# Two layers of a three-branch diffusion backbone: merging the branches straight from PSUM, and the last modulation tiles computed by matrix products

## The chip, the cores and the metric

The kernel runs on one core of one Trainium2 chip. The metric is device time in microseconds (us) of one execution, median of several runs. Smaller is better. The engines are called by the names of the profile: PE is TensorE's matmul, PEld its weight load, DVE is VectorE, ACT is ScalarE, POOL is GpSimd, SP is SyncE, which here only issues DMAs.

## The reference, cut to what matters

Per layer (there are two), on 640 tokens of 1024 channels (128 context tokens, 512 latent tokens):

```python
mod = jnp.einsum('bd,de->be', jax.nn.silu(cond), p['w_mod']) + p['b_mod']
sh1, sc1, g1, sh2, sc2, g2 = jnp.split(mod[:, None, :], 6, axis=-1)
h = rms_norm(x, p['norm1']) * (1 + sc1) + sh1
u_f, q_g, k_g, v_g, r_g, a_g, q_d, k_d, v_d, gates = split_projection(h @ p['w_in'])
y_f = fourier_mix(u_f) @ p['w_fou']
...
y_g = o_g.reshape(b, t, GLA_V) @ p['w_gla_o']
...
y_d = o_d.reshape(b, t, DIFF_V) @ p['w_diff_o']
gf, gg, gd = jnp.split(jax.nn.sigmoid(gates), N_BRANCH, axis=-1)
merged = gf * y_f + gg * y_g + gd * y_d
x = x + g1 * (merged @ p['w_out'])
h2 = rms_norm(x, p['norm2']) * (1 + sc2) + sh2
ff = (jax.nn.silu(h2 @ p['w_ff_gate']) * (h2 @ p['w_ff_up'])) @ p['w_ff_down']
x = x + g2 * ff
```

`mod` has 48 tiles of 128 numbers for each of two conditions (context and latent tokens).

## The kernel before

**Products.** All activations lie channel-major: a tile has 128 channels in the partitions and 640 tokens, cut into two halves of 320 (`SPLIT`). Each float32 operand is split into a high and a low part, and a product is three matmuls (high x high, low x high, high x low). So a gate tile (1024 input channels) is 8 x 3 = 24 matmuls of 320 columns for each half (`group`), and a branch's output tile (512 input channels) is 12. Their results go to the PSUM tiles `main`, of which there are two. A third matmul group can start only when the first one's `main` tile has been read for the last time.

**Weights.** SP loads a raw half unit (L403), ACT rounds it to the high part (L450), POOL subtracts to get the low part (L454). `used` frees a half unit and at once starts this chain for a later one, so a new raw load waits until POOL has emptied a raw buffer.

**The branches' merge.** The mixer runs branch 0 (Fourier), 1 (gated linear attention) and 2 (differential attention). In branches 0 and 1, `branch` alternates for each of 8 output tiles: gate tile (two groups of 24 matmuls, tanh by ACT at L1417), then `merge` (two groups of 12). In branch 2 all 8 gate tiles come first and then all 8 merges. `merge` copies the product out of PSUM with ACT (`y`, L1426); DVE then multiplies by the gate (L1428 in branch 0, L1430 in the others) and, in the others, adds to `merged` (L1431). In branch 2 the sum is also split for the next product: ACT rounds it (`mh`, L485), DVE subtracts (`ml`, L486). The next product is `w_out`, whose first group needs all 8 tiles `mh` of one half.

**Side work.** Attention, linear attention and the Fourier transform are Python generators; `slot(columns)` is called after each group and steps them, so their PE instructions lie between the groups and their DVE instructions are handed out among the merge's.

**Modulation.** A second generator, `back`, is stepped every `rate` columns of main work. Tiles 0 to 15 of a layer are matrix products (`mod_first`, L734, four 32-column parts of the array at once, then a transpose at L743). Tiles 16 to 47 are dot products on DVE: `mod_next` loads `cond_b` (4 DMAs), applies silu to it, and then for each tile loads two half rows (L774) and runs two multiply-and-sum instructions on each (L781) and a final add (L785). In the mixer of layer 0 it makes tiles 16 to 35 and then, from the gates of branch 2 on, 36 to 47 at a rate of 128; in layer 1 it makes 32 to 47 there at a rate of 256. `finish_back` runs what is left of a generator at once.

**Order.** PE's instructions stay in the order in which the program writes them, everywhere (`ORDERED`). From `w_out` to the end of a layer DVE, ACT and POOL do too. In the mixer a planner with its own cost table orders DVE, ACT, POOL and SP; each engine then runs that list in order, and an instruction that waits holds up those behind it.

Of the kernel before, what the change touches and what calls it, by code (L numbers as in the profile page):

```python
# [17 lines left out]
ALU = mybir.AluOpType  # L18
# [4 lines left out]
P = 128  # L23
D = 1024
DEPTH = 2
# [4 lines left out]
KT = D // P  # L30
# [14 lines left out]
UNITS = 58  # L45

AHEAD = 6
ORDERED = {mybir.EngineType.PE}
FFN_ORDERED = {mybir.EngineType.DVE, mybir.EngineType.Activation, mybir.EngineType.Pool}
STEP = 250  # L50
# [73 lines left out]
def weight_jobs():  # L124
# [3 lines left out]
    for l in range(DEPTH):  # L128
        u, pairs = U_FF, set()
        for fp, (_, n) in enumerate(FF_PARTS):  # L130
            pairs.update(range(u + (0 if fp else AHEAD), u + 2 * n, 2))
            u += 3 * n
# [19 lines left out]
def pack_mod(w):  # L152

    return w[:, :2048].reshape(KT, P, 2, 4, 256).transpose(3, 0, 1, 2, 4).reshape(32, P, 512)


def pack_modt(w):

    return w.T.reshape(48, P, 2, 512).transpose(0, 2, 1, 3).reshape(96, P, 512)
# [58 lines left out]
S_N1, S_N2, S_BM, S_GLA, S_DIF = 0, 8, 16, 64, 192  # L218
# [5 lines left out]
def _rows(*vs):  # L224
    return np.concatenate([np.broadcast_to(v.reshape(1, -1), (P, v.size)) for v in vs], 1)


def pack_small(i, l):
    return np.concatenate(
        [  # L230
            i["norm1"][l].reshape(KT, P).T,
            i["norm2"][l].reshape(KT, P).T,
            i["b_mod"][l].reshape(48, P).T,
            _rows(i["gla_norm"][l], i["diff_norm"][l]),
        ],
        1,
    )


def pack_dif(i, l):  # L240
    half = np.arange(64).reshape(2, 2, 16)[:, ::-1].reshape(64)
    gq, gk = i["diff_qk_norm"][l]
    return _rows(gq, gq[half], gk, gk[half], i["diff_lambda"][l])


def pack_a2(i, l):


    w = i["w_gla_a2"][l]
    a, b = np.zeros((P, 4, P), w.dtype), np.zeros((P, 4, P), w.dtype)  # L250
    for pr in range(2):
        for d in range(2):
            s = slice(pr * P, pr * P + P)
            for r in range(d * 16, P, 32):
                a[r : r + 16, pr * 2 + d] = w[d][:, s]
            b[:64:32, pr * 2 + d] = i["b_gla_a"][l][d, s]
    return np.concatenate([a, b])


def layout(i):  # L260
    i = {k: np.asarray(v) for k, v in i.items()}
    x = np.concatenate([i["x_prompt"][0], i["x_sample"][0]], 0)
    cond = np.stack([i["c_ctx"], i["c"][0]], 1)
    return {
        "x_t": np.ascontiguousarray(x.T),
        "cond": np.ascontiguousarray(cond.reshape(KT, P, 2).transpose(1, 0, 2)),
        "w": np.stack([u for l in range(DEPTH) for u in pack_layer(i, l)]),
        "cond_b": np.broadcast_to(cond.T.reshape(1, 2, D), (P, 2, D)),
        "w_mod": np.concatenate([pack_mod(i["w_mod"][l]) for l in range(DEPTH)]),
        "w_modt": np.concatenate([pack_modt(i["w_mod"][l])[32:] for l in range(DEPTH)]),  # L270
        "small": np.stack([pack_small(i, l) for l in range(DEPTH)]),
        "dif": np.stack([pack_dif(i, l) for l in range(DEPTH)]),
        "a2": np.stack([pack_a2(i, l) for l in range(DEPTH)]),

        "ck": np.concatenate([i["cache_diff_k"][0].reshape(DEPTH, P, 2, 4, 64).transpose(0, 2, 4, 3, 1)] * 2, 2),
        "cv": np.ascontiguousarray(i["cache_diff_v"][0].reshape(DEPTH, P, 512)),
        "s0": np.ascontiguousarray(
            i["state_gla"][0].reshape(DEPTH, 2, 2, 2, 64, P).transpose(0, 3, 4, 2, 1, 5).reshape(DEPTH, P, 2, 2, P)
        ),
        **CONST,  # L280
    }
# [23 lines left out]
class Kernel:  # L305
# [446 lines left out]
    def mod_next(self, l, m0, m1, small, mod):  # L752

        nc = self.nc
        cond = {}
        for i in range(2):
            for k in range(2):
                cond[i, k] = self.unit("cond")[:, :512]
                nc.sync.dma_start(cond[i, k], self.a["cond_b"][:, i, k * 512 : (k + 1) * 512])
        yield  # L760
        ends = collections.deque()
        for i, k in [(i, k) for i in range(2) for k in range(2)] + [(None, None)]:
            if i is not None:
                ends.append(self.silu(cond[i, k], self.unit("cond_t")[:, :512]))
            if i is None or len(ends) > 1:
                ends.popleft()()
            yield
        todo = [(m, k) for m in range(m0, m1) for k in range(2)]
        raws = collections.deque()
        for n in range(len(todo) + 2):  # L770
            if n < len(todo):
                m, k = todo[n]
                raws.append(self.unit("rawm")[:, :512])
                nc.sync.dma_start(raws[-1], self.a["w_modt"][l * 64 + m * 2 + k - 32])  # L774
            if n >= 2:
                m, k = todo[n - 2]
                raw = raws.popleft()
                if k == 0:
                    sums = self.sm([P, 2, 2], "modsum", 3)
                for i in range(2):  # L780
                    nc.vector.scalar_tensor_tensor(  # L781
                        self.sm([P, 512], "junk", 1, mybir.dt.bfloat16), raw, 1.0, cond[i, k], op0=ALU.mult, op1=ALU.mult, accum_out=sums[:, i, k : k + 1]
                    )
                if k:
                    nc.vector.scalar_tensor_tensor(mod[:, m], sums[:, :, 0], small[:, S_BM + m : S_BM + m + 1], sums[:, :, 1], op0=ALU.add, op1=ALU.add)  # L785
            yield

    def mod_scale(self, mod, small, gain, tile0, name):

        o = self.lp.tile([P, KT, 2], F32, tag=name, name=self.name(name), bufs=2)  # L790
        for i in range(2):
            self.nc.vector.scalar_tensor_tensor(
                o[:, :, i], mod[:, tile0 : tile0 + KT, i], 1.0, small[:, gain : gain + KT], op0=ALU.add, op1=ALU.mult
            )
        return o
# [624 lines left out]
    def merge(self, l, u, m, act, tg, merged, first=False, parts=None):  # L1420

        nc = self.nc
        for s in SPLIT:
            ps = self.group(self.weight(l, u), (m % 2) * 4, 4, act, s)
            y = self.unit("y")[:, s]
            nc.scalar.copy(y, ps)  # L1426
            if first:
                nc.vector.scalar_tensor_tensor(merged[m][:, s], tg[:, s], 1.0, y, op0=ALU.add, op1=ALU.mult)  # L1428
            else:
                nc.vector.scalar_tensor_tensor(tg[:, s], tg[:, s], 1.0, y, op0=ALU.add, op1=ALU.mult)  # L1430
                nc.vector.tensor_add(merged[m][:, s], merged[m][:, s], tg[:, s])  # L1431
            if parts:
                self.split(merged[m][:, s], parts[0][:, s], parts[1][:, s])
            if m % 2 and s.start:
                self.used(l, u)
            self.slot((s.stop - s.start) // 2)
# [43 lines left out]
    def mixer(self, l, h, small, backs, norms):  # L1480
        nc = self.nc
# [38 lines left out]
        for s in SPLIT:  # L1520
            ps = self.main()[:, : s.stop - s.start]
# [9 lines left out]
        for i, r in enumerate((slice(0, P), slice(P, 2 * P))):  # L1531
            raw, x = (self.unit("a2", t)[:, :512] for t in (F32, F32R))
# [6 lines left out]
        for pr in range(2):  # L1539
            k, q, vs = self.qkv(l, pr, h)  # L1540
# [13 lines left out]
        for pr in range(2):  # L1554
# [14 lines left out]
            if pr == 0:  # L1569
                merged = [self.unit("mg") for _ in range(KT)]  # L1570
# [2 lines left out]
                self.finish(gens[1])  # L1573
                self.branch(l, 1, h, gact, merged)
        self.finish_back()
        self.back, self.rate = backs[1], 128 if l == 0 else 256
        tg = [self.gate(l, U_BR[2] + m, h) for m in range(KT)]
        self.finish(gens[3])
        mg, x2 = self.pairs("m", KT), [self.unit("x2") for _ in range(KT)]
# [7 lines left out]
    def ffn_start(self, l, h2, combine, norms, pair):  # L1587

        us = range(U_FF, U_FF + AHEAD)
        first, second = self.first_four(l, us[:4], h2, norms)  # L1590
        acts = [pair(f) for f in range(AHEAD // 2)]
        for f in range(2):
# [16 lines left out]
        self.used(l, us[2])  # L1609
        for i in range(4, AHEAD):  # L1610
            for p in range(2):
# [86 lines left out]
    def run(self):  # L1698
        nc = self.nc
        self.load_consts()  # L1700
        small, mod = self.load_small(0)
# [3 lines left out]
        with self.tc.manual_schedule(engines={mybir.EngineType.SP}):  # L1705
# [6 lines left out]
            raws = [self.mod_load(0)]  # L1712
# [7 lines left out]
        h = self.pairs("h", KT)  # L1720
        todo = collections.deque()
# [50 lines left out]
        norms = None  # L1772
        for l in range(DEPTH):
            last = l == DEPTH - 1
            if l:
                small, mod = later[l - 1]
            later_mod = lambda a, b: self.mod_next(l, a, b, small, mod)
            mg, x2 = self.mixer(l, h, small, (None, later_mod(32, 48)) if l else (later_mod(16, 36), later_mod(36, 48)), norms)

            g1 = self.lp.tile([P, KT, 2], F32, tag="g1", name=self.name("g1"), bufs=1)  # L1780
            nc.vector.tensor_scalar_mul(g1, mod[:, 16:24, :], 0.5)
# [5 lines left out]
            norms = []  # L1787
# [8 lines left out]
            with self.tc.manual_schedule(engines=FFN_ORDERED):  # L1796
                for m, p in NORM_ORDER:
                    s = SPLIT[p]
# [17 lines left out]
            first, keep, norms = norms, [], []  # L1816
# [13 lines left out]
            h = keep[0]  # L1830
# [3 lines left out]
def hybrid_dit_kernel(ctx: ExitStack, tc: tile.TileContext, a):  # L1834
    with tc.manual_schedule(engines=ORDERED):
        Kernel(ctx, tc, a).run()
# [34 lines left out]
```

## Time and profile before

| | |
|---|---|
| median of 3 runs | 2377.06 us (2373.94 to 2380.15) |
| the profiled execution's own time | 2375.32 us |
| its span, first to last instruction | 2373.5 us |
| PE busy | 2236.4 us, 94% of the span |
| DVE busy | 1639.4 us, 69% |
| ACT busy | 996.0 us, 42% |
| POOL busy | 976.0 us, 41% |
| mean granted TensorE clock | 0.978 of full speed |

PE is the engine that is nearly always busy, so time is lost where PE waits and spent where PE is given more work. The others count where they make PE wait.

### The profile page before, as it was taken

What the parts mean: (1) busy time and instruction counts of PE and PEld (TensorE: products, weight loads), DVE (VectorE), ACT (ScalarE), POOL (GpSimd) and SP (SyncE); (2) the same over time, 40 slices, a digit from 0 to 9 for tenths busy, and PEclk for the clock granted to TensorE, in tenths of its full rate; (3) what the DMA queues carried; (4) which work ended last, traced back from release to release, by engine and by line L of the source; (5) the groups of instructions that cost most, each with busy time, mean ns of one, the idle gap of its engine ahead of it and who ended that gap; (6) DMA issues with size and microseconds to landing.
All of it is one profiled execution on the core that took longest, in us unless ns stands there. A gap on an engine that the chain in (4) does not pass through costs nothing. (4 is left out here: it accounts for less than half of the span.)

```text
span 2373.5 us, 44461 instructions
## 1 busy us (share of the span) xinstructions
PE 2236.4 (94%) x16882; PEld 2187.4 (92%) x16882; DVE 1639.4 (69%) x3386; ACT 996.0 (42%) x2194; POOL 976.0 (41%) x795
## 2 busy tenths in 40 slices
PE   6988899999999899998989999999998998999999
PEld 4978799999999899998989899999998988999999
DVE  5796877686955857778763657867748667575674
ACT  3444445454235424241434554464633254242332
POOL 1344544353333634342533545524433255252533
PEclk9999999999999999999999999999999999999999
DMA  7443221112622272836242222212135322424433
GB/s 269 161 128 102 72 74 59 56 57 76 222 84 81 87 246 85 274 111 211 88 142 72 79 72 72 70 37 76 50 108 182 129 90 74 158 93 162 138 103 125
DMA packets 151381, 271.39 MB, mean 114 GB/s; under 512 B 19200, under 2 KB 31360, under 8 KB 151168
## 3 DMA queue, kind: packets, MB, share of 16 engines
q1 hardware_dynamic: 125824, 219.75, 28.4%
q10 hardware_dynamic: 25344, 48.80, 5.9%
q8 instruction: 133, 2.18, 0.4%
q14 instruction: 80, 0.66, 0.1%
HBM read 235.98 MB, written 27.79 MB: 111 GB/s over the span
## 5 line engine op out<-in xcount | busy, mean ns | idle before, releaser
L454 POOL TENSOR_TENSOR wl<-raw,wh 128x512 fp32r<-128x512 f32 x514 | 707.6, 1391 | 1055.8 <-ACT wh L450 890.1
L450 ACT CAST wh<-raw 128x512 fp32r<-128x512 f32 x518 | 314.9, 619 | 295.6 <-PE main L492 161.9
L492 PE MATMUL main<-hh,wh 128*128 128x320 f32 x936 | 294.9, 315 | 0.8 <-DVE aT L1526 0.8
L492 PE MATMUL main<-hh,wl 128*128 128x320 f32 x936 | 289.5, 309 | 0.0
L492 PE MATMUL main<-hl,wh 128*128 128x320 f32 x936 | 289.5, 309 | 0.0
L492 PE MATMUL main<-wh,hh 128*128 128x256 f32 x800 | 236.8, 296 | 9.0 <-DVE rx L1472 4.9
L781 DVE SCALAR_TENSOR_TENSOR junk<-rawm,cond 128x512 bf16<-128x512 f32 x256 | 222.8, 870 | 27.6 <-DMA rawm<-in_w_modt_dram 22.8
L492 PE MATMUL main<-wl,hh 128*128 128x256 f32 x800 | 230.8, 289 | 0.0
L492 PE MATMUL main<-wh,hl 128*128 128x256 f32 x800 | 230.7, 288 | 0.0
L492 PE MATMUL main<-ah,wh 128*128 128x320 f32 x704 | 219.9, 312 | 7.0 <-DVE x L1453 5.4
L1453 DVE SCALAR_TENSOR_TENSOR x<-main,g,x 128x128 f32<-128x128 f32 (+2 forms) x240 | 97.3, 435 | 185.9 <-PE main L492 170.6
L492 PE MATMUL main<-al,wh 128*128 128x320 f32 x704 | 217.5, 309 | 0.0
L492 PE MATMUL main<-ah,wl 128*128 128x320 f32 x704 | 217.5, 309 | 0.0
L450 ACT CAST wh<-big 128x512 fp32r<-128x512 f32 x152 | 89.2, 587 | 261.1 <-DVE big L433 74.6
L492 PEld LDWEIGHTS main<-hh,wh 128*128 128x128 f32 x936 | 176.4, 188 | 1.6 <-DVE aT L1526 1.0
L492 PE MATMUL main<-h2h,wh 128*128 128x320 f32 x520 | 165.8, 319 | 12.7 <-DVE tt L297 6.3
L492 PEld LDWEIGHTS main<-hl,wh 128*128 128x128 f32 x936 | 176.4, 188 | 0.1
L492 PEld LDWEIGHTS main<-hh,wl 128*128 128x128 f32 x936 | 176.0, 188 | 0.0
L492 PEld LDWEIGHTS main<-wh,hh 128*128 128x128 f32 x800 | 158.3, 198 | 11.8 <-DVE rx L1472 5.1
L492 PE MATMUL main<-h2l,wh 128*128 128x320 f32 x520 | 164.6, 317 | 0.0
L492 PE MATMUL main<-h2h,wl 128*128 128x320 f32 x520 | 164.5, 316 | 0.0
L492 PEld LDWEIGHTS main<-wl,hh 128*128 128x128 f32 x800 | 158.2, 198 | 0.0
(359 smaller groups left out, 6152.7 us busy)
## 6 DMA issues: line engine op xcount, KB each, us to landing
raw<-in_w_dram SPq DMA_DIRECT2D x556, 256.0 KB, 2.9
rawm<-in_w_modt_dram SPq DMA_DIRECT2D x128, 256.0 KB, 4.6
x<-xd ACTq DMA_DIRECT2D x64, 320.0 KB, 4.5
rawm<-in_w_mod_dram SPq DMA_DIRECT2D x64, 256.0 KB, 5.4
xd<-x ACTq DMA_DIRECT2D x48, 320.0 KB, 4.1
xd<-x ACTq DMA_DIRECT2D x48, 160.0 KB, 2.0
cond<-in_cond_b_dram SPq DMA_DIRECT2D x16, 256.0 KB, 4.5
x<-in_x_t_dram SPq DMA_DIRECT2D x12, 320.0 KB, 5.1
```

The lines of the kernel that those rows point to most:

```text
L450: nc.scalar.copy(h, raw)
L454: (nc.vector if late or sums else nc.gpsimd).tensor_sub(lo, raw, h.bitcast(F32))
L492: mm = lambda w, x, first=False, last=False: nc.tensor.matmul(ps, w, x, start=first and not more, stop=last, skip_group_check=more)
L781: nc.vector.scalar_tensor_tensor(self.sm([P, 512], "junk", 1, mybir.dt.bfloat16), raw, 1.0, cond[i, k], op0=ALU.mult, op1=ALU.mult, accum_ ...
L1453: nc.vector.scalar_tensor_tensor(x[:, r], ps[:, r.start - s.start : r.stop - s.start], g[:, m, i : i + 1], x[:, r], op0=ALU.mult, op1=ALU.add)
```

## The change

`merge` no longer copies: DVE multiplies the gate with the PSUM tile itself. In branch 0 it writes `merged`; in branches 1 and 2 it writes the product back into the same PSUM tile and then adds that to `merged`. Tiles 36 to 47 of layer 0 and 32 to 47 of layer 1 become matrix products in a new generator, `mod_rows`, with weights in a new layout (`w_modr`). Four tiles take two halves of four loads (256 KB each) and 16 matmuls each, then a copy by ACT and a transpose. The rate from the gates of branch 2 on is 640 in both layers.

```diff
+MOD_ROWS = (36, 32)
+MOD_BLOCKS = tuple((48 - m) // 4 for m in MOD_ROWS)
...
+    def mod_rows(self, l, m0, m1, small, mod):
+        nc = self.nc
+        todo = [(m, half) for m in range(m0, m1, 4) for half in range(2)]
+        raws = collections.deque()
+        for n in range(len(todo) + 1):
+            if n < len(todo):
+                m, half = todo[n]
+                raws.append([self.unit("rawm")[:, :512] for _ in range(4)])
+                for k, raw in enumerate(raws[-1]):
+                    nc.sync.dma_start(raw, self.a["w_modr"][((m - m0) // 4 + sum(MOD_BLOCKS[:l])) * KT + 4 * half + k])
+                yield
+            if n:
+                m, half = todo[n - 1]
+                if half == 0:
+                    ps = self.misc()
+                for k, raw in enumerate(raws.popleft()):
+                    for j in range(4):
+                        nc.tensor.matmul(
+                            ps[32 * j : 32 * j + 32, :P], self.cond[:, 4 * half + k, :], raw[:, j * P : (j + 1) * P],
+                            start=(half + k == 0), stop=(half == 1 and k == 3),
+                        )
+                if half:
+                    row = self.sm([P, P], "row", 2)
+                    nc.scalar.copy(row, ps[:, :P])
+                    yield
+                    ps = self.misc()
+                    nc.tensor.transpose(ps[:, :P], row, self.c("ident"))
+                    src = ps[:, :P].rearrange("p (m i) -> p m i", m=4)[:, :, :2]
+                    nc.vector.tensor_add(mod[:, m : m + 4], src, small[:, S_BM + m : S_BM + m + 4, None].to_broadcast([P, 4, 2]))
+                yield
...
             ps = self.group(self.weight(l, u), (m % 2) * 4, 4, act, s)
-            y = self.unit("y")[:, s]
-            nc.scalar.copy(y, ps)
             if first:
-                nc.vector.scalar_tensor_tensor(merged[m][:, s], tg[:, s], 1.0, y, op0=ALU.add, op1=ALU.mult)
+                nc.vector.scalar_tensor_tensor(merged[m][:, s], tg[:, s], 1.0, ps, op0=ALU.add, op1=ALU.mult)
             else:
-                nc.vector.scalar_tensor_tensor(tg[:, s], tg[:, s], 1.0, y, op0=ALU.add, op1=ALU.mult)
-                nc.vector.tensor_add(merged[m][:, s], merged[m][:, s], tg[:, s])
+                nc.vector.scalar_tensor_tensor(ps, tg[:, s], 1.0, ps, op0=ALU.add, op1=ALU.mult)
+                nc.vector.tensor_add(merged[m][:, s], ps, merged[m][:, s])
...
-        self.back, self.rate = backs[1], 128 if l == 0 else 256
+        self.back, self.rate = backs[1], 640
...
-            later_mod = lambda a, b: self.mod_next(l, a, b, small, mod)
-            mg, x2 = self.mixer(l, h, small, (None, later_mod(32, 48)) if l else (later_mod(16, 36), later_mod(36, 48)), norms)
+            first_mod = self.mod_next(l, 16, MOD_ROWS[l], small, mod) if l == 0 else None
+            mg, x2 = self.mixer(l, h, small, (first_mod, self.mod_rows(l, MOD_ROWS[l], 48, small, mod)), norms)
```

## Rows read from the trace of the kernel before

**Rows 1.** The page, busy time of each engine.
```profile
PE 2236.4 (94%) x16882; PEld 2187.4 (92%) x16882; DVE 1639.4 (69%) x3386; ACT 996.0 (42%) x2194; POOL 976.0 (41%) x795
```

**Rows 2.** PE's waits, whole span: who waited for whom, total us, times, longest.
```profile
PE main L492 <- ACT y L1426: 14.9, 11, 3.8
...
PE big L1340 <- POOL q L1324: 6.4, 4, 1.7
...
PE main L492 <- ACT mh L485: 5.2, 2, 4.1
...
PE big L1282 <- DVE kT L1238: 3.1, 2, 1.5
```

**Rows 3.** Busy time by stretch: us, PE, PEld, DVE, ACT, POOL, granted clock, DMA.
```profile
639.65:676.70 37.05, 31.27 (x194) 29.69 (x193) 31.46 (x62) 16.19 (x38) 11.61 (x9) 0.95 0.33 111
...
1807.65:1848.52 40.87, 31.68 (x194) 29.72 (x193) 36.05 (x82) 15.61 (x37) 11.50 (x9) 0.96 0.47 159
1848.52:1864.00 15.48, 11.43 (x58) 10.78 (x57) 12.74 (x35) 2.69 (x6) 1.38 (x1) 0.78 0.60 213
...
1751.50:1807.50 56.00, 56.00 (x383) 56.00 (x383) 36.66 (x67) 18.10 (x36) 21.20 (x16) 1.00 0.48 162
```

**Rows 4.** DVE in order of time, the last merge of layer 1: start, duration.
```profile
1853.92 0.48 DVE L1430 SCALAR_TENSOR_TENSOR tg<-tg,y 128x320 f32<-128x320 f32 x1
1854.33 0.68 DVE L781 SCALAR_TENSOR_TENSOR junk<-rawm,cond 128x512 bf16<-128x512 f32 x1
...
1854.94 0.48 DVE L1431 TENSOR_TENSOR mg<-mg,tg 128x320 f32<-128x320 f32 x1
```

**Rows 5.** Groups of DVE instructions by shape: count, busy us, mean ns, idle before.
```profile
L781 DVE SCALAR_TENSOR_TENSOR junk<-rawm,cond 128x512 bf16<-128x512 f32 x256 | 222.8, 870 | 27.6 <-DMA rawm<-in_w_modt_dram 22.8
...
L1430 DVE SCALAR_TENSOR_TENSOR tg<-tg,y 128x320 f32<-128x320 f32 x64 | 41.5, 652 | 7.8 <-ACT y L1426 7.7
L1431 DVE TENSOR_TENSOR mg<-mg,tg 128x320 f32<-128x320 f32 x64 | 38.2, 601 | 1.2
```

**Rows 6.** The instructions of L595: ns min/median/max, first and last start.
```profile
L595 DVE SCALAR_TENSOR_TENSOR tt<-tt,main x38: 475/477/478, 809.0 to 2331.2; 128x320 f32<-128x320 f32 x38
```

**Rows 7.** Modulation matmuls between others, then at the start of the kernel.
```profile
865.54 0.31 PE L492 MATMUL main<-ah,wl 128*128 128x320 f32 x1
865.78 1.08 PE L734 MATMUL misc<-rawm,cond 128*32 128x128 f32 x32
866.79 0.41 PE L492 MATMUL main<-ah,wh 128*128 128x320 f32 x1
...
19.65 0.65 PE L734 MATMUL misc<-rawm,cond 128*32 128x128 f32 x8
...
20.69 0.47 PE L743 MATMUL misc<-const,row 128*128 128x128 f32 x1 [0.39 <-ACT row L740]
```

**Rows 8.** SP at the end of layer 1's merges; DMAs there: KB, us to landing.
```profile
1852.46 0.33 SPq L403 DMA_DIRECT2D raw<-in_w_dram  x1
1852.88 4.11 SPq L774 DMA_DIRECT2D rawm<-in_w_modt_dram  x8
...
rawm<-in_w_modt_dram SPq DMA_DIRECT2D x8, 256.0 KB, 4.4
```

**Rows 9.** DVE's merge instruction and PE's next gate: first, worst, last late pair.
```profile
325.31 0.31 PE L492 MATMUL main<-hh,wh 128*128 128x320 f32 x1
...
325.50 0.48 DVE L1428 SCALAR_TENSOR_TENSOR mg<-tg,y 128x320 f32<-128x320 f32 x1
...
359.50 0.39 PE L492 MATMUL main<-hh,wh 128*128 128x320 f32 x1
...
366.84 0.47 DVE L1428 SCALAR_TENSOR_TENSOR mg<-tg,y 128x320 f32<-128x320 f32 x1
...
1739.85 0.49 DVE L1431 TENSOR_TENSOR mg<-mg,tg 128x320 f32<-128x320 f32 x1
...
1740.23 0.31 PE L492 MATMUL main<-hh,wh 128*128 128x320 f32 x1
```

More of the change, by code (lines that the diff above doesn't have):

```diff
@@ L154, in pack_mod, with pack_modr @@
     return w[:, :2048].reshape(KT, P, 2, 4, 256).transpose(3, 0, 1, 2, 4).reshape(32, P, 512)
+def pack_modr(w, m0):
+    return w[:, P * m0 :].reshape(KT, P, -1, 512).transpose(2, 0, 1, 3).reshape(-1, P, 512)
 def pack_modt(w):
@@ L270, in layout @@
         "w_modt": np.concatenate([pack_modt(i["w_mod"][l])[32:] for l in range(DEPTH)]),
+        "w_modr": np.concatenate([pack_modr(i["w_mod"][l], MOD_ROWS[l]) for l in range(DEPTH)]),
         "small": np.stack([pack_small(i, l) for l in range(DEPTH)]),
```

## Prediction

> **What bounds the kernel now.** I read the page first: PE is busy 94% of the span, DVE 69%, ACT 42% [rows 1]. So a us is won only where PE waits, and each matmul that is added costs its own time. Next come PE's waits by cause [rows 2]: the merge's ACT copy costs 14.9 us in 11 waits, and the rounding `mh` at the start of `w_out` 5.2 in two. Narrowed to stretches, all of both lies in the merges of branch 2 and just behind them; in branches 0 and 1 PE waits for the merge nowhere. There the two waits on side work appear, 6.4 and 3.1 us over both layers.
>
> Then the stretches [rows 3]. Branch 2's gates, at full clock and without a wait, take 56.0 us for 16 groups of 24 matmuls, the last row of the group; its merges are 16 groups of 12 and would need half, 28.0 us. They take 37.05 us in layer 0 and 40.87 in layer 1: 9.0 + 12.8 = 21.8 us lost, part of it at a reduced granted clock (0.95 and 0.96 over the stretch). Behind them come the 5.2 us for `mh`, about 1.4 in short steps of the same two groups, and in layer 1 a clock of 0.78 over 15.48 us, which is 0.22 x 15.48 = 3.4 us. Together 10.0.
>
> The order of time at the end of layer 1 shows why [rows 4]: between the merge's multiply at 1853.92 and its add at 1854.94 DVE runs a modulation instruction of 0.68 us, and `mh` and PE stand behind that add.
>
> **Part 1, modulation on PE.** It removes 112 half rows: 24 + 32 from the two tile counts, times two, so 2 x (24 + 32) = 112 instructions of L781 at 0.870 us, 97 us of DVE [rows 5], and the second loading and silu of `cond_b`. None of it is on PE. It adds, for 3 + 4 blocks of two halves, 14 sets of 16 matmuls. The trace lists such a matmul twice: 32 records are one set, and PE goes from 865.54 to 866.79 over it [rows 7], 1.25 us where the next matmul would have come 0.147 later: 1.10 us a set, 15.4 us in all. A transpose between other matmuls costs 0.03, so **+15.6**. Nothing hides this: PE was not waiting in the gates.
>
> **Part 2, branch 2's merges.** DVE has three instructions a half left: multiply, add, `ml`. Reading PSUM costs no more than reading SBUF: an instruction of the same kind and size with one operand in PSUM takes 477 ns, never above 478 [rows 6], where the merge's two on SBUF take 652 and 601 on average [rows 5], slow ones beside POOL's subtractions. So a half needs about 0.48 + 0.48 + 0.5 = 1.5 us of DVE against PE's 1.76, and ACT no longer holds a copy behind a rounding that waits for DVE. Where POOL runs beside it, `ml` can still take some 1.3 and pass a half us to PE, once in every few halves: I keep 2 us a layer (0 to 21.8 in both together as bounds): **-17.8**. The `w_out` waits of 10.0 go: the last rounding is done about 1.7 us after the last merge matmul, while `w_out` needs it only after 21 matmuls, 3.1 us: **-10.0**.
>
> The Trainium skill speaks against this part: Perfetto Trace Analysis, Optimizing Scalar/DVE Operations, gives a DVE instruction some 125 ns of access time on PSUM against some 60 on SBUF, and VectorE: DVE Perf Modes, Rules for kernel authors, advises copying a matmul's result to SBUF first when many operations follow. By that, an estimate: 160 instructions (64 + 64 + 32) x 0.065 = 10 us more DVE time, some 2 us of it where PE waits, and the sum below would end 2 us higher; the row of L595 shows no such surcharge.
>
> **Part 3, what is left at `finish_back`.** Gates and merges give 8 x 640 + 8 x 320 = 7680 columns, 12 steps at 640. Layer 0 has 15 steps (6 loads, 6 sets, 3 transposes), layer 1 has 20. So after the last merge PE still meets two sets and a transpose in layer 0, four sets and two transposes in layer 1, all in a row and ahead of `w_out`. (What is left from the previous rate can bring one step forward in layer 1.) Two costs. First, each transpose now follows its set at once and waits for ACT's copy: in the first block of the kernel that is 20.69 - 19.65 - 0.24 = 0.80 us from the last matmul, where 0.20 is usual [rows 7]: 3 x 0.6 = 1.8. Second, the last loads. SP runs its list in order; at this place of layer 1 the modulation loads stood behind a weight load that was issued 3.9 us after the last merge matmul (at 1848.5), eight of them took 4.1 us to issue and 4.4 to land each [rows 8]. If layer 0's last four and layer 1's last eight are issued that late, their sets wait until about 8 to 10 us after the merges, less the 1 to 2 us of sets that PE can do meanwhile: 7 us in each layer, and the clock falls again as it did behind waits of this length. If they are issued during the merges, nothing. Bounds 1.8 and 21; I take **+10**, since the row is of the same place but the list will be made anew.
>
> **Part 4, branches 0 and 1.** Here the copy protected PE. ACT freed the `main` tile 0.4 us after the group; now DVE frees it, and DVE is behind. PE needs the tile of a merge's first half again when the second half is done, 1.76 us later plus any side matmuls. I compared, for all 32 pairs, the end of DVE's last merge instruction with PE's next group on that tile. It is later in 18 pairs, 9 in each layer; first 325.98 against 325.31, worst 367.3 against 359.50, last 1740.34 against 1740.23 [rows 9]. The worst has DVE working off query and key preparation for 8 us. Added up as they stand it is 18.8 us a layer. Stepping through DVE's list with PSUM durations, and with PE's delay handed on so that DVE catches up meanwhile, leaves 13.4. In the same stretches PE's own waits on that side work, 6.4 + 3.1 = 9.5 us over both layers [rows 2], would be absorbed, since what it waits for goes on during the new ones: 13.4 - 4.7 = 8.7 a layer, **+17.4**. Bounds: 37.6 with nothing caught up; on the other side -9.5, if the multiplies, ready sooner, move ahead in the list and the relieved DVE even removes those waits.
>
> **Sum:** 15.6 - 17.8 - 10.0 + 10 + 17.4 = +15.2 us on the profiled execution's 2375.3, that is 2390.5. The median of the runs lies 1.7 above that execution: **2392**.
>
> **Rivals.** (a) *DVE keeps ahead in branches 0 and 1.* For it: DVE loses 19 us of duration in the merge (64 x 0.175 + 64 x 0.12, [rows 5, 6]), and each multiply is ready half a us sooner. Against it: at the worst place DVE has 8 us of older work, which no half us overtakes. With part 4 at -9.5 the sum is -11.7: 2365. It decides from part 4 below -5 for faster. (b) *The two halves cancel:* part 4 between -5 and +9, or part 3 near its lower bound with part 4 at 10: about 2377. For it: the list is made anew with PE visibly waiting on DVE. (c) *Branch 2 does not gain:* the late loads cost their full 21 and `ml` beside POOL holds the merges at half of today's loss: -10.9 in place of -17.8, +21 in place of +10, sum 15.6 - 10.9 - 10.0 + 21 + 17.4 = +33: 2410. Against it: 1.5 us of DVE a half against 1.76. (d) *The wait only moves* from the copy to DVE's add in branch 2, so that the merges keep all 21.8: 15.2 + 17.8 = +33 too, 2410; then DVE would have been the bound all along.
>
> **How the numbers follow.** The forecast, slower by 0.4 to 1.3%: 0.46. (a) 0.20, (b) 0.24, (c) and (d) together 0.10. A change under 0.3% (7 us) is about what a measurement here can't tell from none. So faster 0.20, same 0.24, slower 0.56. The range that leaves out 2 in 10 is 2364 to 2414; that of the forecast alone is 2384 to 2408.
>
> **What would show it.** Right: 448 more records of misc<-rawm,cond, 15 us busy; waits of PE's `main` on the DVE lines of the merge, 10 us or more, nearly all between 310 and 580 and 1480 and 1740, the longest near 360 and 1527; branch 2's merges at about 30 us a layer; SP issuing the last `w_modr` loads after the last merge, and PE waiting for them 3 to 8 us a layer. Wrong: if PE's waits on the merge in branches 0 and 1 sum to under 8 us, part 4 fails; if `w_out` starts within 5 us of layer 1's last merge, part 3 does; if branch 2's merges stay above 34 us, part 2.

## The result, and the profile after

The changed kernel takes 2388.91 us, median of four runs (2380.97 to 2390.74), where the kernel before took 2376.18 beside it (four runs, 2373.94 to 2380.15). The ratio is 1.0055, 95% interval 1.0037 to 1.0074: 12.7 us slower.

The page of after, busy time of each engine, against [rows 1]:

```profile
PE 2241.4 (94%) x17337; PEld 2187.4 (92%) x17337; DVE 1493.7 (63%) x3125; ACT 962.4 (40%) x2097; POOL 969.7 (41%) x795
```

DVE lost 146 us and ACT 34. Had their busy time been what counts, the kernel would be faster. PE's busy time grew by 5.0 us and the span by 5.7. But busy time also shrinks where the clock is higher (see below), so these totals do not tell what the change cost; its waits and the stretches do. After's waits of PE over the whole span, against [rows 2] (who waited for whom, total us, times, longest):

```profile
PE main L501 <- DVE mg L1467: 13.4, 10, 4.8
...
PE misc L815 <- DMA rawm<-in_w_modr_dram: 9.5, 7, 3.7
...
PE main L501 <- DVE mg L1470: 5.0, 6, 1.6
...
PE big L1323 <- DVE kT L1279: 3.1, 2, 1.5
...
PE misc L824 <- ACT row L821: 1.2, 3, 0.4
```

The waits for ACT's copy (14.9) and for `mh` (5.2) are gone, and so is the 6.4 for POOL's `q`. In their place stand 18.4 us for DVE's merge (L1467 is the multiply of branch 0, L1470 the add of the others), 9.5 for the modulation's loads and 1.2 for the row's copy. By stretch, from the row of gates in layer 0 to the end of `w_out` in layer 1, columns as in [rows 3]:

```profile
589.80:649.84 60.04, 60.04 (x483) 58.86 (x482) 1.40 (x5) 17.02 (x34) 21.06 (x17) 1.00 0.47 154
649.84:679.90 30.06, 29.91 (x229) 29.07 (x225) 21.60 (x45) 10.73 (x23) 10.35 (x8) 1.00 0.50 162
679.90:690.00 10.10, 4.58 (x70) 2.68 (x70) 2.18 (x6) 1.39 (x4) 1.39 (x1) 0.70 0.44 151
690.00:749.60 59.60, 58.26 (x395) 57.94 (x395) 23.08 (x56) 17.75 (x39) 17.34 (x14) 0.99 0.29 95
1757.50:1817.70 60.20, 60.20 (x484) 59.02 (x483) 1.15 (x3) 16.07 (x32) 20.47 (x16) 1.00 0.47 159
1817.70:1847.70 30.00, 29.85 (x227) 28.98 (x225) 21.88 (x47) 11.68 (x25) 11.01 (x9) 1.00 0.53 181
1847.70:1861.10 13.40, 8.18 (x135) 4.46 (x135) 2.36 (x7) 1.71 (x5) 1.41 (x1) 0.76 0.63 207
1861.10:1922.00 60.90, 59.55 (x395) 59.23 (x395) 22.90 (x56) 17.65 (x39) 17.21 (x14) 0.97 0.28 93
```

The gates (first and fifth row) are as full as before and 4 us longer. The merges (second and sixth) fell from 37 and 41 us to 30, with DVE busy 21.6 and 21.9 us in place of 31 and 36. Behind each of them is a stretch that did not exist before, 10.1 and 13.4 us in which PE is idle for 5 us and the granted clock is 0.70 and 0.76.

To compare stretch by stretch I took, from PE's records, the starts of the first and the last matmul of each kind of work, and subtracted. Branches 0 and 1 run from the first merge matmul to the last, "gates of branch 2" from branch 1's last one to branch 2's first, and "tail" from the last merge matmul of branch 2 to the first matmul of `w_out`.

| us | layer 0: before, after | layer 1: before, after | both |
|---|---|---|---|
| branch 0 | 98.22, 104.14 | 98.16, 103.99 | +11.8 |
| branch 1 | 106.88, 107.56 | 106.88, 107.56 | +1.4 |
| gates of branch 2 | 56.47, 60.08 | 56.47, 60.18 | +7.3 |
| merges of branch 2 | 36.90, 29.84 | 40.73, 29.82 | -18.0 |
| tail | 0.15, 9.35 | 0.15, 12.61 | +21.7 |
| `w_out` | 60.93, 60.02 | 66.73, 61.40 | -6.25 |
| sum | | | +17.9 |

The profiled execution of after took 2380.97 us, the shortest of its four and only 5.7 above that of before, though the touched stretches are 17.9 longer. The missing 12 lie in work that the change does not touch, from `w_out` of layer 0 to branch 0 of layer 1. The same windows of before and of after:

```profile
737.60:1477.90 740.30, 699.64 (x5508) 683.41 (x5506) 501.92 (x954) 303.01 (x619) 325.65 (x257) 0.97 0.39 126
```

```profile
749.00:1477.70 728.70, 691.10 (x5508) 675.11 (x5506) 501.96 (x954) 302.90 (x619) 326.35 (x257) 0.98 0.40 128
```

As many matmuls, 11.6 us less. Summed over the clock's records (a stretch at the 1.2 GHz level counts half its length as lost), time lost there is 22.2 us before and 11.9 after. After's three other runs (2387 to 2391) have mean clocks of 0.976 to 0.978, like before's; the profiled one has 0.982. So I read the effect of the change from the stretches it touches, and the time from the medians. The two do not quite meet: the medians are 12.7 us apart, the touched stretches 17.9. Where the runs that were not profiled differ from the profiled one is not shown.

### The profile page after: what moved, and what is told of

Read it like the earlier page. It is cut to its first block, busy times and chain, and to the rows that moved or that the text cites. A ratio compares the mean times of both kernels' runs of the same rounds, so it can differ in the third digit from the quotient of the medians.

```text
span 2379.2 us, 44929 instructions
## 1 busy us (share of the span) xinstructions
PE 2241.4 (94%) x17337; PEld 2187.4 (92%) x17337; DVE 1493.7 (63%) x3125; ACT 962.4 (40%) x2097; POOL 969.7 (41%) x795
## 4 chain that ended last, share of the span: by engine, by line
PE 55%; DVE 9%; issue 2%; ACT 2%; POOL 2%; DMA 1%; SPq 0%; ACTq 0%; DVEq 0%; POOLq 0%
PE main L501 39%; PE misc L501 8%; PE big L527 1%; DVE w L1313 1%; PE main L527 1%; DVE junk L790 1%; PE misc L1432 1%; PE big L1381 1%; DVE x L1492 1%; ACT wh L459 1%; POOL wl L463 1%; PE big L1089 0%; PE misc L815 0%; POOL ek L1168 0%; DVE wl L463 0%
## 5 line engine op out<-in xcount | busy, mean ns | idle before, releaser
L501 PE MATMUL main<-hh,wh 128*128 128x320 f32 x936 | 297.6, 318 | 18.2 <-DVE mg L1467 13.4
L501 PE MATMUL main<-h2h,wh 128*128 128x320 f32 x520 | 165.2, 318 | 14.4 <-DVE tt L306 6.4
L501 PEld LDWEIGHTS main<-wh,hh 128*128 128x128 f32 x800 | 156.4, 196 | 12.7 <-ACT tm L653 5.6
L501 PEld LDWEIGHTS main<-wh,hl 128*128 128x128 f32 x800 | 156.1, 195 | 0.0
```

The source lines that it names most:

```text
L501: mm = lambda w, x, first=False, last=False: nc.tensor.matmul(ps, w, x, start=first and not more, stop=last, skip_group_check=more)
```

## The experiments

Times stand beside runs of the kernel before on the same chip (medians 2373.31, 2373.71 and 2370.96 in three sessions). Stretches are taken as in the table above.

**1. The copy back in branches 0 and 1 alone** (`copy01`). Theory: without the copy, DVE's backlog reaches PE there. (`parts` is given in branch 2 only.)

```diff
-            if first:
+            if not parts:
+                y = self.unit("y")[:, s]
+                nc.scalar.copy(y, ps)
+                if first:
+                    nc.vector.scalar_tensor_tensor(merged[m][:, s], tg[:, s], 1.0, y, op0=ALU.add, op1=ALU.mult)
+                else:
+                    nc.vector.scalar_tensor_tensor(tg[:, s], tg[:, s], 1.0, y, op0=ALU.add, op1=ALU.mult)
+                    nc.vector.tensor_add(merged[m][:, s], merged[m][:, s], tg[:, s])
+            elif first:
```

> The changed kernel, with ACT's copy back in the merges of branches 0 and 1 alone (branch 2 still reads PSUM). Theory (DVE frees the main tile too late there): the two branches of both layers lose their 13.1 us of added length, branch 0 going back from 104 to 98.2 us a layer and branch 1 from 107.6 to 106.9; total about 13 us under the changed kernel, close to the kernel before (ratio 0.998 to 1.003). Rival (the 15.6 us of added matmuls and the tail are the whole loss, and a wait removed in branch 0 comes back at the side work behind it): within 3 us of the changed kernel, ratio 1.004 to 1.007.

Measured 2373.65 us, ratio 0.9999 (0.9988 to 1.0010). Branches 0 and 1 are back at the times of before (within 0.05 us, one of them 1.5 shorter by a clock that did not fall). Gates and merges stay as in after. The direct read costs 13 us there (1.0055 to 0.9999) and gains nothing. Its longest wait in after, PE and then DVE in order of time:

```profile
361.16 0.38 PE L1358 MATMUL misc<-const,y 128*128 128x128 f32 x2
366.33 0.44 PE L501 MATMUL main<-hh,wh 128*128 128x320 f32 x1 [4.79 <-DVE mg L1467]
```

```profile
361.78 2.46 DVE L1313 TENSOR_TENSOR w<-xn,tab 128x64 f32<-128x64 f32 x4
364.16 0.28 DVE L1307 TENSOR_TENSOR y<-xn,tab 128x128 f32<-128x128 f32 x1
364.71 0.43 DVE L1314 TENSOR_TENSOR y<-y,w 128x256 f32<-128x256 f32 x1 [0.27 <-DVE y L1307]
365.06 0.82 DVE L1313 TENSOR_TENSOR w<-xn,tab 128x64 f32<-128x64 f32 x4
365.80 0.47 DVE L1467 SCALAR_TENSOR_TENSOR mg<-tg,main 128x320 f32<-128x320 f32 x1
```

PE has nothing to do from 361.5 on; the merge's multiply runs at 365.80, behind query and key preparation. In the kernel before it ran as late, at 366.84 [rows 9], but there ACT had emptied the tile and PE went on at 359.50.

**2. The modulation stepped sooner** (`rate384`): the same work, but every load and set issued ahead of the end of branch 2.

```diff
-        self.back, self.rate = backs[1], 640
+        self.back, self.rate = backs[1], 384
```

> The changed kernel with the rate at 384 columns a step in place of 640, so that all 15 and 20 steps of the modulation fall into the gates and merges and nothing is left behind the last merge. Theory (the last loads are issued after the merges and PE stands waiting for them): the stretch from the last merge to w_out, 9.35 and 12.6 us, falls to under 2 us in each layer; the same 14 sets of matmuls cost their 1.1 us earlier, 6 of them inside the merges' stretches; total about 15 us under the changed kernel, ratio to before 0.997 to 1.001. Rival (loads come as late whatever step issues them, since SP is behind weight loads or no unit is free): PE waits for them inside the merges instead, and the total is within 4 us of the changed kernel.

Measured 2373.14 us, ratio 0.9995 (0.9985 to 1.0006). Both tails are 0.15 us again, the gates 6.1 and 6.2 longer than before (they hold five sets in place of three), `w_out` 59.1 in both layers. So 14 us of the loss (1.0055 to 0.9995) hang on one number, the rate. What it cost can be seen in after, at the end of layer 1, SP and then PE:

```profile
1846.43 0.33 SPq L412 DMA_DIRECT2D raw<-in_w_dram  x1
1846.86 0.38 SPq L807 DMA_DIRECT2D rawm<-in_w_modr_dram  x1
1849.93 0.33 SPq L412 DMA_DIRECT2D raw<-in_w_dram  x1
1850.35 4.05 SPq L807 DMA_DIRECT2D rawm<-in_w_modr_dram  x7
```

```profile
1854.32 0.43 PE L815 MATMUL misc<-rawm,cond 128*32 128x128 f32 x8 [2.47 <-DMA rawm<-in_w_modr_dram]
1855.04 0.66 PE L815 MATMUL misc<-rawm,cond 128*32 128x128 f32 x8 [0.29 <-DMA rawm<-in_w_modr_dram]
1856.33 3.24 PE L815 MATMUL misc<-rawm,cond 128*32 128x128 f32 x40 [0.63 <-DMA rawm<-in_w_modr_dram]
1860.01 0.47 PE L824 MATMUL misc<-const,row 128*128 128x128 f32 x1 [0.44 <-ACT row L821]
1860.14 0.62 PE L501 MATMUL main<-mh,wh 128*128 128x320 f32 x1
```

The merges end at 1847.5. SP issues the last seven loads at 1850.35, behind a weight load, and `w_out` starts at 1860.14 behind the last transpose. The weight loads themselves wait for POOL, as before the change: 10.4 us in four waits of SP between 1838 and 1868 (22.1 before).

**3. Both cures** (`both`): the edits of 1 and 2 together.

> Both: ACT's copy back in branches 0 and 1, and 384 columns a step. Theory: the two add up, 13 + 15 us under the changed kernel, ratio to before 0.992 to 0.996: branch 2's shorter merges (18 us) and the earlier w_out outweigh the 15.6 us of matmuls. Rival (added matmuls are the loss): no faster than before, ratio 0.999 or more.

Measured 2357.22 us (2355.02 to 2362.82), ratio 0.9936 (0.9924 to 0.9948): 16 us faster than the kernel before. The two cures add up (0.0056 and 0.0060 of the ratio singly, 0.0119 together), so the two losses were independent of each other.

**4. The copy in all merges** (`copy_all`): the modulation on TensorE at rate 640, ACT's copy back in branch 2 too.

> The changed kernel with ACT's copy back in every merge, so that only the modulation's move to TensorE is left of the change. Theory: branches 0 and 1 as before; the tails of 9.35 and 12.6 us stay; branch 2's merges lie between 29.8 and 37 to 41 us, near 33, since DVE's modulation instructions are gone but ACT's in-order copy behind a rounding stays; total 5 to 9 us under the changed kernel, ratio 1.001 to 1.004. Rival (the copy cost nothing in branch 2, DVE's modulation did all of it): merges at 30 us, total 13 us under the changed kernel. Other rival (the copy was all of it): merges stay at 37 to 41.

Measured 2386.95 us, ratio 1.0057 (1.0045 to 1.0069), above what I expected. Against `copy01` the merges are 4.9 and 5.3 us longer and the tails 3.1 in sum. In the trace:

```profile
PE main L501 <- ACT y L1467: 7.4, 11, 0.9
```

As many waits as before the change [rows 2], but 7.4 us in place of 14.9, and the longest 0.9 in place of 3.8. So the copy still costs 5 us a layer with the modulation off DVE, and what the copies save in branches 0 and 1 is spent again here and in the tails.

**5. The halves apart, without the two losses.** `direct_b2`: the kernel before with the direct merge in branch 2 only. `mod_pe`: the kernel before with the modulation on TensorE at rate 384 only. `direct_all`: the kernel before with the direct merge in all three branches.

> The kernel before with the merge edit in branch 2 alone: copies stay in branches 0 and 1, the modulation stays on DVE at its old rates. Theory: branches 0 and 1 as before, merges of branch 2 and w_out as in direct_all, so direct_all minus 13 us: 0.991 to 0.995 of the kernel before, and within 5 us of the kernel that has both cures (0.9936), since the 15.4 us that the sets cost PE are saved and the modulation's instructions on DVE give back less than half of the gain. Rival (the copy alone caused branch 2's loss): merges 29.8 in both layers, 0.988 or less. Other rival (the modulation alone caused it): 0.998 to 1.000.

> The kernel before with the modulation on TensorE alone, at rate 384, and ACT's copy in all merges: the modulation edit without the merge edit. Theory: branches 0 and 1 as before; sets cost 15.4 us on PE, all of them in gates and merges, none behind the merges; merges without sets about 32 to 33 us a layer (the copy still costs 3 to 5); w_out within 2 us of 59. Sum +15.4 - 4 - 8 - 10 = about -6: 0.995 to 1.000. Rival (removing DVE's modulation instructions is what frees branch 2): merges without sets at 28 to 29 us, ratio 0.994 as with both cures, so that the merge edit is worth nothing.

> The kernel before with the merge edit alone: all three branches' merges read PSUM directly; the modulation stays on DVE at its old rates, nothing is added to PE. Theory (branches 0 and 1 pay 13.1 us for the copy, whatever the modulation does; in branch 2 the copy and the modulation's DVE instructions both held PE up): branches 0 and 1 longer by 6.6 us a layer as in the changed kernel; gates of branch 2 and the stretch in front of w_out as before (0.15 us); branch 2's merges about 30 us in layer 0 and 33 to 36 in layer 1, where 12 or more modulation instructions of 0.87 us still fall into the merges; w_out 3 to 6 us shorter. Sum +13.1 - 7 - 6 - 4 = about -4: 0.997 to 1.001 of the kernel before. Rival (the modulation's DVE instructions alone cause branch 2's loss): merges stay at 36 and 40, ratio 1.005.

| | ratio (95%) | merges of branch 2, layers 0 and 1 | `w_out` |
|---|---|---|---|
| before | 1 | 36.90, 40.73 | 60.93, 66.73 |
| `direct_b2` | 0.9957 (0.9942 to 0.9973) | 38.52, 39.15 | 59.12, 60.31 |
| `mod_pe` | 0.9972 (0.9960 to 0.9984) | 32.63, 34.76 | 60.94, 60.92 |
| `both` | 0.9936 (0.9924 to 0.9948) | 29.42, 31.84 | 59.12, 59.11 |
| `direct_all` | 1.0020 (1.0008 to 1.0031) | 37.42, 39.42 | 59.12, 60.31 |

(With the modulation on PE the merges hold one set in layer 0 and three in layer 1.) `mod_pe` came as the theory said in its ratio; its merges without sets are 31.4 and 31.1 us, a little under the 32 to 33 expected. The other two missed, in the merges and in the ratio: I expected the direct merge alone to bring the merges to 30 and to 33 to 36 us, and their sum did not change; of the stretches only `w_out` is clearly shorter (8.2 us in both layers). Why, in `direct_b2`, layer 0, DVE and then PE:

```profile
650.09 0.69 DVE L781 SCALAR_TENSOR_TENSOR junk<-rawm,cond 128x512 bf16<-128x512 f32 x1
650.71 0.08 DVE L781 DVE_READ_ACCUMULATOR junk<-rawm,cond 128x1 f32 x1
650.82 0.22 DVE L785 SCALAR_TENSOR_TENSOR mod<-modsum,small 128x2 f32<-128x2 f32 x1
651.08 0.17 DVE L1789 TENSOR_SCALAR g<-mod 128x16 f32<-128x16 f32 x1
651.16 0.49 DVE L1436 SCALAR_TENSOR_TENSOR main<-tg,main 128x320 f32<-128x320 f32 x1
651.69 0.49 DVE L1437 TENSOR_TENSOR mg<-main,mg 128x320 f32<-128x320 f32 x1
```

```profile
652.24 0.63 PE L492 MATMUL main<-dh,wh 128*128 128x320 f32 x1 [6.97 <-DVE mg L1437]
```

The two merge stretches of `direct_b2`, columns as in [rows 3]:

```profile
641.60:680.20 38.60, 31.48 (x194) 30.77 (x193) 29.30 (x66) 11.42 (x24) 11.61 (x9) 0.87 0.32 102
1802.60:1841.80 39.20, 30.77 (x194) 28.08 (x192) 37.57 (x89) 10.98 (x23) 11.35 (x9) 1.00 0.53 175
```

In layer 0 DVE still works off modulation when the first merge comes; with no copy in between PE waits 7.0 us for it, and the granted clock over these merges is 0.87. In layer 1 the modulation instructions stand between the merges, 16.45 us of them in 39.2 us, and DVE is busy nearly throughout (37.57 us). That is the mechanism of branches 0 and 1 once more. `direct_all` less `direct_b2` is 13.8 us, the loss of branches 0 and 1 without any part of the modulation's edit.

**6. Layer 0's DVE backlog spread out** (`spread_l0`): `direct_b2` with layer 0's rate at 192 in place of 128.

> The kernel with the direct merge in branch 2 alone, with layer 0's modulation rate 192 in place of 128, so that some 6 of its 48 DVE instructions move from the gates into the merges. Theory (the 7 us that PE waits after layer 0's first two merges is DVE's backlog of modulation at that moment, and the half clock behind it follows from it): the wait falls to 3 us or less, layer 0's merges from 38.5 to 31 to 35 us, the rest unchanged: 0.9935 to 0.995 of the kernel before. Rival (DVE has more work in gates and merges together than PE, wherever it stands): layer 0's merges stay at 37 us or more, 0.9955 to 0.997.

Measured 2362.16 us, ratio 0.9954 (0.9937 to 0.9971): no better, and with merges of 39.7 us the rival's outcome. From matmul to matmul the first gap halves (3.4 us after the first two merge groups in place of 7.3), and another of 3.5 us comes 17 us later. So at this rate the wait only moves. That no rate would do better is not shown: DVE is busy for 76 of the 96 us of gates and merges here, and for 77 of 95 in `direct_b2`.

**7. The loads two halves ahead** (`early_loads`): the changed kernel, its loop one step longer.

```diff
-        for n in range(len(todo) + 1):
+        for n in range(len(todo) + 2):
...
-            if n:
-                m, half = todo[n - 1]
+            if n > 1:
+                m, half = todo[n - 2]
```

> The changed kernel with the modulation's loads two halves ahead of their sets in place of one; as many steps, the same order of everything else. Theory (PE waits behind the merges for loads that were issued behind a weight load): in layer 0 all loads now come before the 12th step, so what is left behind the merges is two sets and a transpose, 2 to 3.5 us in place of 9.4; in layer 1 four sets and the last two half loads are still behind the merges, 8 to 13 us in place of 12.6. Together 6 to 9 us less than the changed kernel: about 1.002 to 1.004 of the kernel before. Rival (the loads wait for a free unit, or the sets and transposes themselves take the time): layer 0 keeps 7 us or more, ratio 1.005 to 1.007.

Measured 2380.36 us, ratio 1.0036 (1.0023 to 1.0049), as the theory said. Layer 0's tail falls from 9.35 to 2.77 us, though two sets and two transposes stand in it; layer 1's, whose last seven loads are still issued at 1850.20, stays at 12.29. So it is the late loads more than the sets that make the tail.

**8. A quarter of each set** (`quarter_sets`): `both` with 4 of 16 matmuls in each set; the last modulation tiles are then sums over two of eight parts.

```diff
                 for k, raw in enumerate(raws.popleft()):
+                    if k != 3 * half:
+                        continue
```

> The kernel with both cures (copies in branches 0 and 1, direct merge in branch 2, modulation on TensorE at rate 384), with 4 of the 16 matmuls of each modulation set; the other 12 are left out, so that the last modulation tiles sum over 2 of 8 parts. Loads, copies, transposes and all else stay. Theory (each matmul of a set costs PE its own time, 1.10 us a set, and nothing covers it): 14 x 1.10 x 12/16 = 11.6 us less than with both cures, 0.987 to 0.990 of the kernel before; gates of branch 2 come down from +6.1 to about +1.5 in each layer. Rival (the sets stand where PE would wait anyway, so that they cost little): less than 5 us off, 0.9915 or more.

Measured 2350.70 us, ratio 0.9901 (0.9879 to 0.9923); the stretches of branch 2 are 6.9 us shorter than in `both`, where I expected 11.6. A set in `both`, then in `quarter_sets`:

```profile
598.32 0.31 PE L501 MATMUL main<-hh,wl 128*128 128x320 f32 x1
598.56 1.08 PE L815 MATMUL misc<-rawm,cond 128*32 128x128 f32 x32
599.57 0.41 PE L501 MATMUL main<-hh,wh 128*128 128x320 f32 x1
```

```profile
601.63 0.31 PE L501 MATMUL main<-hh,wl 128*128 128x320 f32 x1
601.87 0.43 PE L817 MATMUL misc<-rawm,cond 128*32 128x128 f32 x8
602.23 0.42 PE L501 MATMUL main<-hh,wh 128*128 128x320 f32 x1
```

1.25 us from main matmul to main matmul with the whole set, 0.60 with a quarter: 12 matmuls are worth 0.65, not 0.83. By these two points (an estimate) a matmul of a set costs 0.054, and going in and out 0.24 whatever the set holds: 0.60 - 4 x 0.054 - 0.147, the usual step between main matmuls. 14 x 0.65 = 9.1. The gates show it (five sets in each layer, 3.28 us less, 0.66 a set); in the merges, where 2.6 us less were to come, only 0.3 did: PE runs into DVE there, with one wait of 0.9 and one of 0.8 us on the add that `both` does not have.

## Why the prediction was right

2388.9 was measured for a forecast of 2392, and the forecast was the case that came: the gain in branch 2 is real, and what it costs elsewhere is more. The mechanisms came as told; that the sum comes so near is in part luck, since the terms are off by 1.4 to 4.4 us in both directions. By its steps, each in us over both layers:

| term | predicted | measured in the stretches |
|---|---|---|
| part 1, 14 sets on PE | +15.6 | +17.0 |
| part 2, merges of branch 2 | -17.8 | -20.4 |
| part 2, `w_out` | -10.0 | -6.25 |
| part 3, tail without its six sets | +10 | +14.4 |
| part 4, branches 0 and 1 | +17.4 | +13.1 |
| sum | +15.2 | +17.9 |

**Part 1** was sized from a set between two main matmuls, 1.10 us. The gates of after (three sets each and a transpose) give 7.3 / 6 = 1.22, because the matmul behind a set is late as well (0.41 us where 0.31 is usual). With 1.21 for the other eight it is 7.3 + 9.7 = 17.0; nothing hid them, as was said.

**Part 2, merges.** 18.0 shorter with two sets of 1.21 in them, so 20.4 for the rest; 2.6 more than forecast, as PE lost next to nothing (29.91 of 30.06 us busy) where I had kept 2 us a layer for `ml`. That DVE would need only 1.5 us a half was right: 21.6 us for 16 halves and what lies beside. But the prediction counted DVE's list without modulation and ACT's without the copy, and did not ask which of the two brings the gain. `direct_b2` and `mod_pe` do: alone, the direct merge gains nothing in the merges, and the modulation on PE gains 5.5 and 9.6 us, its one and three sets taken off; together (`both`) they gain 8.7 and 12.5. Rival (d), that the wait only moves to DVE's add, is what the direct merge does without the other half.

The Trainium skill's rule that was weighed there (Perfetto Trace Analysis, Optimizing Scalar/DVE Operations: some 125 ns of access on PSUM against 60 on SBUF) would, by the prediction's estimate, have made each instruction 65 ns longer. The trace does not agree. After's three merge instructions, then the three that they replace:

```profile
L1467 DVE SCALAR_TENSOR_TENSOR mg<-tg,main x32: 469/478/490, 312.9 to 1582.1; 128x320 f32<-128x320 f32 x32
...
L1469 DVE SCALAR_TENSOR_TENSOR main<-tg,main x64: 481/495/497, 485.5 to 1847.9; 128x320 f32<-128x320 f32 x64
...
L1470 DVE TENSOR_TENSOR mg<-main,mg x64: 478/491/492, 486.1 to 1848.7; 128x320 f32<-128x320 f32 x64
```

```profile
L1428 DVE SCALAR_TENSOR_TENSOR mg<-tg,y x32: 473/491/1592, 313.3 to 1578.8; 128x320 f32<-128x320 f32 x32
...
L1430 DVE SCALAR_TENSOR_TENSOR tg<-tg,y x64: 475/484/1570, 480.3 to 1853.9; 128x320 f32<-128x320 f32 x64
...
L1431 DVE TENSOR_TENSOR mg<-mg,tg x64: 472/491/1591, 480.8 to 1854.9; 128x320 f32<-128x320 f32 x64
```

(ns min/median/max.) The median is 11 ns longer at most, and the longest is under a third: 497 against 1592.

**Part 2, `w_out`,** was mis-sized. Layer 1's 66.73 fell to 61.40 and not to the 59.1 of `rate384`, since behind the new wait in front the granted clock is lower again (0.76 and 0.97 in the last two rows by stretch): time lost at 1.2 GHz in `w_out` is 0.9 and 2.4 us, by the clock's records. That belongs to part 3. Without these, the term is 6.25 + 3.3 = 9.6.

**Part 3** was right in its mechanism and low in size. The loads that were to be late are late, by the weight load that was named, in both layers. Of the tails' 21.7 us six sets are 7.3 (at 1.21 each, an estimate), so 14.4 are waits and low clock, inside the bounds of 1.8 and 21; with `w_out`'s 3.3 it is 17.7. `rate384` removes all of it, `early_loads` that of layer 0.

**Part 4** was right in its mechanism too, and a little high. PE waits for the merge 9.0 us a layer in branches 0 and 1, where the stepping gave 13.4, and of the 4.7 that were to be absorbed 3.2 are (POOL's `q`; `kT` keeps its 1.5 a layer). After's waits of PE from 302 to 590 us, layer 0; layer 1 has the same sums:

```profile
PE main L501 <- DVE mg L1467: 6.7, 5, 4.8
PE main L501 <- DVE mg L1470: 2.3, 2, 1.6
PE big L1323 <- DVE kT L1279: 1.5, 1, 1.5
```

9.0 - 3.2 = 5.8, and the stretches grew by 6.6. The longest wait is at the place that was named, 366.33 and 1534.04. PE is stopped seven times in each layer. The prediction's count of late pairs, nine a layer and 18.8 us, is too low: by its own rule the trace of before has eleven a layer and 26.7 us. One of those left out comes right behind the pair that it calls the last, PE's group and then DVE's add:

```profile
1743.75 0.31 PE L492 MATMUL main<-hh,wh 128*128 128x320 f32 x1
```

```profile
1744.61 0.49 DVE L1431 TENSOR_TENSOR mg<-mg,tg 128x320 f32<-128x320 f32 x1
```

So the upper bound of 37.6 was too low as well; the forecast went by the stepping, which was a little high. That each stop gives DVE time to catch up before the next is the likely reason why so much less than the count came; it was not measured by itself.

**The rivals.** (a) falls by `copy01`: DVE does not keep ahead. (b) falls by the interval of the ratio, whose lower end is 1.0037; it would have come true with either loss cured, as `copy01` and `rate384` show at 1.000. (c) is half true: of its 21 us for the loads 14.4 to 17.7 came, its slow merges did not.

Open stays whether the modulation has a place that costs neither PE nor DVE anything. `both`, the fastest run that leaves nothing out, still pays 14 sets on PE; `direct_b2` pays none and is some 5 us slower (0.9957 against 0.9936, from two sessions, with intervals that just overlap), since DVE then holds PE up instead.

## What to carry to other kernels

A copy out of PSUM by an engine with time to spare is a buffer between PE and an engine that runs late: before it is removed, compare, pair by pair, when the late engine would free the bank with when PE asks for it again, and remove it only where that engine has been relieved. A generator that is stepped by columns must have issued its last load well before the work it is spread over ends; count its steps against the columns, and look at what stands in front of its loads in the queue. Here each of two small choices (which branches, which rate) cost 13 to 14 us, nearly as much as the 16 that the change could gain.

## What the runs showed of the hardware

DVE instructions with an operand in PSUM did not stretch beside POOL: none of 160 in after took over 497 ns, where the 160 with all operands in SBUF that they replaced reached 1592. Of those, 29 took over 600 ns, and every one of the 29 had POOL at work for more than half of its time; of the 160 in after POOL was at work for more than half of the time of 54, and they were no longer than the rest. With the PSUM operand they are also the shorter ones on average, by [rows 5]: 652 and 601 ns before. The Trainium skill (VectorE: DVE Perf Modes, Two Vector instructions with no wait between them) says that an instruction with two SBUF tensor inputs reads the second through an interface shared with GpSimd; the rows agree with that, and no run here tests it by itself.

The time lost to a lower granted clock in work that a change leaves alone differed by 10 us between two profiled executions (22.2 and 11.9), about as much as several of the differences studied here; stretches of equal content showed it, the total did not.
